# Other PSUM banks under the first attention scores, and two weight splits, two scale operations and two projection steps at other places of the order

## The chip, the cores and the metric

One core of one Trainium2 chip. The metric is the device time of one execution in microseconds (us).

## What is computed

One layer of a hybrid backbone over 512 latent tokens of width 1024, with a prefix of 256 context tokens. Cut to what matters here:

```python
hx = modulate(rms_norm(x), sh1, sc1)            # 512 tokens
hc = modulate(rms_norm(ctx), csh1, csc1)        # 256 tokens
ak, av, qkv, db, da, aq, z, gate = split_cols(h @ w_in)
q = rope(rms_norm(aq, q_norm_w)); k = rope(rms_norm(ak, k_norm_w))
attn = softmax(q @ k.T * HEAD_DIM**-0.5) @ v    # 8 heads, 2 key/value heads, 768 keys
q, k, v = silu(dwconv_centred(qkv, conv_w))     # gated DeltaNet, 8 heads, two directions
gdn = gdn_output(gdn_bidirectional(...), z)
x = x + g1 * merge_branches(attn, gdn, gate, w_pa, w_pd, w_out)
x = x + g2 * conv_ffn(modulate(rms_norm(x), sh2, sc2), w_up, ..., w_down)
return rms_norm(x, final_norm_w)
```

## The kernel before

Every product is done in three matmuls of split numbers: a weight arrives as `wraw`, ACT rounds it to `whi`, DVE takes the rest to `wlo` (`load_w`, L199; two raw buffers, three of each half), and the activations are kept in halves likewise (names ending in H and L).

PSUM has eight banks. Two (`mb`) and one (`xb`) belong to the whole program; the `xb` bank is a single one that every transposition outside the stages goes through. The other five go to one stage after the other. In the stage ahead of the key/query stage they are two `pt`, a `pm` and two `pc`. In the key/query stage (L669 to L753) they are three `pq` (the projection of a tile of 128 tokens) and two `pt` (its transposes). In the attention (L757 to L850) they are one score tile `pS` of two banks and three `ab` (transposed probabilities and values). A stage's pool gives out its banks in the order in which the code first asks for each tag.

The key/query stage has six blocks, for keys, values and four times two query heads, of six, six and four times four tiles. A tile's `pq` is accumulated in 24 matmuls; ACT squares it for the norm, DVE rotates it (`rope`, L678, six operations that read `pq` and one that adds) into `qt`, and three tiles later PE transposes `qt` into `pt` (`columns`, L688; `pend` holds what is still to be transposed). The last three tiles of the last block are transposed inside the attention, through `xb`. After a block of queries `rsqrt` and a multiplication make its scales `qsc`: a DVE operation, a power on POOL, a DVE operation.

`attend` (L821) goes through 32 units (8 heads, four tiles of 128 queries). For unit u it puts down the softmax (maximum on DVE, its product with the scale, exp on ACT with the sum, reciprocal and multiplication on DVE), then the scores of unit u + 1, which need the score tile that exp has read, then the transposes of the probabilities of unit u - 1 into `ab` (split on ACT to `PH` and on DVE to `PL`), and after every second unit the 18 value matmuls into `ab` (copied by ACT to `ao`). Between these it yields, and at each yield one step of `fillA` runs on PE: `projections` of the DeltaNet's convolution inputs, eight projections of 12 steps (eight of three 512-wide matmuls, four of six 256-wide ones, all into `mb`). `F0` to `F3` (L68) say how many steps stand at each yield; F0 stands between the first scores and the rest. ACT and DVE take a finished `mb` through the short convolution (`t1`, `co`); some steps later `tokens` (L289) transposes `co` through `xb`, where ACT copies it and squares it in place.

The order on PE is the order of the code (`pinned`). On ACT and DVE a scheduler chooses the order from its own model of times, with priorities (`first`, `sooner`). Each engine then works through its list strictly in that order, waiting at each instruction for what it needs. The load of a projection's weights stands in the program where a `wraw` buffer comes free, and its split where the scheduler puts it.

## Time and profile before

| what | us |
|---|---|
| median of 3 runs | 1256.99 |
| lowest and highest | 1254.07, 1263.17 |
| the profiled execution | 1254.9 |
| its span | 1253.1 |
| PE busy | 1193.0 (95%) |
| DVE busy | 834.0 (67%) |
| ACT busy | 613.8 (49%) |
| attention, from the first score matmul to the end of the last values | 156.31 to 327.57 |

Busy time of PE is the time in which a matmul is under way. A row of the order in time gives the start in us, the length, engine, line, operation and tiles; in brackets at its end stands how long the engine was idle just before, and what ended that. A table by windows gives the busy time and the number of instructions of each engine in a stretch, and the clock granted to TensorE as a share of the full one.

### The profile page before, as it was taken

The numbers are of one execution on the slowest core, as the hardware profiler recorded it, in microseconds if no ns is written. First come the engines' busy times: TensorE is split into PE (matmuls) and PEld (weight loads), VectorE is DVE, ScalarE is ACT, GpSimd is POOL, SyncE is SP. The second block draws the span as 40 slices with busy tenths as digits, with TensorE's granted clock in tenths as the row PEclk, the third lists the DMA queues.
The fourth block names the chain that finished last, engine by engine and source line by source line (L and its number), as shares of the span: only waits on it lengthen the run. The fifth ranks groups of instructions, "written<-read, shape, count | busy, mean of one in ns | idle before, by whom it ended". The sixth has DMA issues, their size and how long they took to land.

```text
span 1253.1 us, 20509 instructions
## 1 busy us (share of the span) xinstructions
PE 1193.0 (95%) x7733; PEld 1015.7 (81%) x7733; DVE 834.0 (67%) x1609; ACT 613.8 (49%) x1403; POOL 274.0 (22%) x347
## 2 busy tenths in 40 slices
PE   6999999999979899999999999999999999999996
PEld 3499879898768688778888678789888888888886
DVE  5666767777689866766757588855776756653333
ACT  6534466666675673773634632333544444442331
POOL 0020110110332387587484200210000000000000
PEclk9999999999999999999999999999999999999998
DMA  9412211211635533543546786763333333223331
GB/s 376 146 60 85 86 60 60 81 60 68 200 112 179 171 115 118 170 147 107 173 143 192 231 292 214 265 213 133 102 134 125 127 101 101 95 86 102 96 93 67
DMA packets 66403, 171.83 MB, mean 137 GB/s; under 512 B 7328, under 2 KB 18048, under 8 KB 64896
## 3 DMA queue, kind: packets, MB, share of 16 engines
q1 hardware_dynamic: 66304, 170.52, 41.0%
q8 instruction: 61, 1.00, 0.3%
q14 instruction: 38, 0.31, 0.1%
HBM read 145.28 MB, written 25.21 MB: 136 GB/s over the span
## 4 chain that ended last, share of the span: by engine, by line
PE 74%; DMA 7%; DVE 6%; POOL 5%; ACT 4%; issue 2%; SPq 0%; POOLq 0%; DVEq 0%; ACTq 0%
PE mc L85 33%; PE mb L85 19%; PE pq L85 6%; PE pb L85 5%; PE pS L85 3%; PE ab L85 3%; PE pm L85 2%; PE ab L89 2%; DVE wlo L106 1%; POOL NN L106 1%; DMA NN<-gamdr 1%; POOL prod L106 1%; DMA Gb<-gamdr 1%; POOL R L106 1%; PE pk L85 1%
## 5 line engine op out<-in xcount | busy, mean ns | idle before, releaser
L106 DVE TENSOR_TENSOR wlo<-wraw,whi 128x1024 fp32r<-128x1024 f32 (+1 forms) x153 | 190.5, 1246 | 150.2 <-ACT whi L118 149.5
L118 ACT ACTIVATE whi<-wraw 128x1024 fp32r<-128x1024 f32 (+1 forms) x153 | 159.6, 1045 | 216.8 <-PE mc L85 112.4
L85 PE MATMUL mc<-h,whi 128*128 128x512 f32 (+1 forms) x752 | 219.9, 376 | 0.3 <-ACT whi L118 0.3
L85 PE MATMUL mb<-hxH,whi 128*128 128x512 f32 x384 | 162.0, 422 | 5.8 <-DVE t L115 3.7
L85 PEld LDWEIGHTS mc<-h,whi 128*128 128x128 f32 x752 | 138.1, 188 | 25.9 <-ACT whi L118 0.5
L85 PE MATMUL mb<-hxH,wlo 128*128 128x512 f32 x384 | 152.0, 396 | 0.0
L85 PE MATMUL mb<-hxL,whi 128*128 128x512 f32 x384 | 151.3, 394 | 0.0
L85 PE MATMUL mc<-h,wlo 128*128 128x512 f32 (+1 forms) x376 | 141.5, 376 | 0.5 <-DVE wlo L106 0.5
L85 PE MATMUL mc<-a,whi 128*128 128x512 f32 (+1 forms) x396 | 111.2, 367 | 0.6 <-DVE x L115 0.6
L106 POOL TENSOR_TENSOR rc<-rc,mhalf 128x2 f32<-128x2 f32 x4 | 3.0, 741 | 407.8 <-DVE rc L112 407.8
L85 PEld LDWEIGHTS mb<-hxH,whi 128*128 128x128 f32 x384 | 73.4, 191 | 16.1 <-ACT t L118 4.4
L85 PEld LDWEIGHTS mb<-hxH,wlo 128*128 128x128 f32 x384 | 72.7, 189 | 16.6
L85 PEld LDWEIGHTS mc<-a,whi 128*128 128x128 f32 x396 | 71.6, 189 | 12.8 <-DVE x L115 0.8
L85 PEld LDWEIGHTS mc<-h,wlo 128*128 128x128 f32 x376 | 70.8, 188 | 13.6 <-DVE wlo L106 1.0
L85 PEld LDWEIGHTS mb<-hxL,whi 128*128 128x128 f32 x384 | 73.3, 191 | 9.5
L85 PE MATMUL mc<-a,wlo 128*128 128x512 f32 (+1 forms) x198 | 72.5, 366 | 0.0
L115 DVE SCALAR_TENSOR_TENSOR u<-mc,col,u 128x511 f32<-128x511 f32 x88 | 65.3, 746 | 1.4
L106 POOL TENSOR_TENSOR R<-R,prod 128x31 f32<-128x31 f32 (+15 forms) x93 | 57.1, 614 | 7.0
L106 POOL TENSOR_TENSOR prod<-X,R 128x31 f32<-128x31 f32 (+15 forms) x93 | 54.1, 582 | 20.2 <-DVE X L106 13.4
L85 PE MATMUL pq<-whi,hxH 128*128 128x256 f32 (+1 forms) x192 | 55.5, 289 | 0.0
L85 PE MATMUL pq<-wlo,hxH 128*128 128x256 f32 (+1 forms) x192 | 54.2, 283 | 0.1
L85 PE MATMUL pq<-whi,hxL 128*128 128x256 f32 (+1 forms) x192 | 54.1, 282 | 0.0
(329 smaller groups left out, 2759.5 us busy)
## 6 DMA issues: line engine op xcount, KB each, us to landing
wraw<-in_w_cm_dram SPq DMA_DIRECT2D x48, 512.0 KB, 3.6
wraw<-in_w_up_dram SPq DMA_DIRECT2D x44, 512.0 KB, 3.3
wl<-in_w_mod_dram SPq DMA_DIRECT2D x24, 512.0 KB, 4.3
wm<-in_w_mod_dram SPq DMA_DIRECT2D x8, 1024.0 KB, 11.2
wraw<-in_w_down_dram SPq DMA_DIRECT2D x16, 512.0 KB, 3.6
wraw<-in_w_aq_dram SPq DMA_DIRECT2D x10, 512.0 KB, 3.8
M<-gamdr SPq DMA_DIRECT2D x64, 64.0 KB, 4.7
wraw<-in_w_pa_dram SPq DMA_DIRECT2D x8, 512.0 KB, 4.4
```

The lines of the kernel that those rows point to most:

```text
L85: i = nc.tensor.matmul(*a, **k)
L89: i = nc.tensor.transpose(*a, **k)
L106: (eng or V).tensor_tensor(out=out, in0=a, in1=b, op=op)
L115: V.scalar_tensor_tensor(out=out, in0=a, scalar=s, in1=b, op0=op0, op1=op1)
L118: A.activation(out, a, f, **kw)
```

## The change

Four things, all at the passage from the key/query stage to the attention:

- The key/query stage asks for one `pt` before its first `pq` (it is used for the first tile's transposes), and the attention asks for one `ab` before its first score tile (it is used for the first probabilities). So `pt` takes the first two of the five banks and `pq` the other three; `ab` takes the first three and `pS` the last two.
- F0 is 5 in place of 3. The number of steps in all stays the same, so two steps fewer are left for the end of the attention.
- The weights of the second and third projection of the attention (`ahead`) are loaded and split after softmax(0) and after softmax(1), in the order of the code on ACT and DVE (`in_order`). In the kernel before, the scheduler had put these splits ahead of the last tile's rotation.
- The scales of the last query block are made in softmax(1) and softmax(2), in place of the end of the key/query stage.

```diff
--- before.py
+++ after.py
@@ -65,7 +65,7 @@
 AP2 = 7
 PIN = 1
 RA = .6
-F0, F1, F2, F3 = 3, 1, 1, 1
+F0, F1, F2, F3 = 5, 1, 1, 1
 AQ, AK, AM, AR = 24, 10, 32, 10
 
 C_ID, C_ONE, C_MS, C_MI, C_TRI = 0, 128, 256, 512, 768
@@ -102,20 +102,31 @@
         if dbg is not None and name in dbg:
             SP.dma_start(dbg[name], ap)
 
+    strict = [False]
+
+    def put(i):
+        return tc.keep_in_program_order(i) if strict[0] else i
+
+    def in_order(fn, *a):
+        strict[0] = True
+        r = fn(*a)
+        strict[0] = False
+        return r
+
     def tt(out, a, b, op, eng=None):
-        (eng or V).tensor_tensor(out=out, in0=a, in1=b, op=op)
+        put((eng or V).tensor_tensor(out=out, in0=a, in1=b, op=op))
 
     def ts(out, a, s1, op0, s2=None, op1=None, eng=None):
         if op1 is None:
-            (eng or V).tensor_scalar(out=out, in0=a, scalar1=s1, scalar2=None, op0=op0)
+            put((eng or V).tensor_scalar(out=out, in0=a, scalar1=s1, scalar2=None, op0=op0))
         else:
-            (eng or V).tensor_scalar(out=out, in0=a, scalar1=s1, scalar2=s2, op0=op0, op1=op1)
+            put((eng or V).tensor_scalar(out=out, in0=a, scalar1=s1, scalar2=s2, op0=op0, op1=op1))
 
     def stt(out, a, s, b, op0, op1):
-        V.scalar_tensor_tensor(out=out, in0=a, scalar=s, in1=b, op0=op0, op1=op1)
+        put(V.scalar_tensor_tensor(out=out, in0=a, scalar=s, in1=b, op0=op0, op1=op1))
 
     def act(out, a, f=AF.Copy, **kw):
-        A.activation(out, a, f, **kw)
+        put(A.activation(out, a, f, **kw))
 
     def split(hi, lo, src):
         act(hi, src)
@@ -275,8 +286,11 @@
                 act(out[:, 0:n], t1[:, 0:n], AF.Tanh, scale=0.5)
                 stt(out[:, 0:n], out[:, 0:n], 1.0, t1[:, 0:n], ALU.add, ALU.mult)
 
-        def conv_proj(tile_idx, out, with_ctx):
-            w = load_w(w_cm[tile_idx])
+        ahead = {}
+        proj_w = lambda i: w_cm[8 * order[i][1] + order[i][0]]
+
+        def conv_proj(tile_idx, out, with_ctx, w=None):
+            w = w or load_w(w_cm[tile_idx])
             off = NCX if with_ctx else 0
             n = off + NL
             t1 = stp.tile([P, NA], F32, name="t1", tag="t1", bufs=2)
@@ -335,9 +349,9 @@
                 late.pop(0)[1]()
                 n -= 1
 
-        def head_proj(h, part):
+        def head_proj(h, part, w=None):
             o = cbuf()
-            yield from conv_proj(8 * part + h, o, part != 0)
+            yield from conv_proj(8 * part + h, o, part != 0, w)
             head_out(h, part, o)
 
         def head_out(h, part, o):
@@ -417,7 +431,7 @@
 
         def projections(i0, i1):
             for i in range(i0, i1):
-                yield from head_proj(*order[i])
+                yield from head_proj(*order[i], ahead.pop(i, None))
 
         tb_es = ExitStack()
         tbp = tb_es.enter_context(tc.tile_pool(name="tbp", bufs=1, side="right"))
@@ -694,6 +708,8 @@
                 hi, lo = (KH, KL) if blk == 0 else (QH[blk - 2], QL[blk - 2])
                 split(hi[:, :, ts_], lo[:, :, ts_], pt)
 
+
+            pt1 = [kps.tile([P, 2, P], F32, name="pt", tag="pt", bufs=2)]
             pend, dec = [], decays(kvp)
             pinned[0] = KPIN
             psc = next(dec)
@@ -715,7 +731,7 @@
                         T.matmul(pq, xl[:, k, sl], hi[:, wsl], start=False, stop=False)
                         T.matmul(pq, xh[:, k, sl], lo[:, wsl], start=False, stop=(k == KT - 1))
                     if len(pend) >= LAG:
-                        columns(*pend.pop(0))
+                        columns(*pend.pop(0), *(pt1.pop() for _ in pt1[:]))
                     if (blk, t) in DAT:
                         next(dec, None)
                     if blk == 1:
@@ -743,7 +759,7 @@
                             for j in range(2):
                                 ts(qt[:, j * 128:j * 128 + 128], qt[:, j * 128:j * 128 + 128], rk[:, j:j + 1], ALU.mult)
                     pend.append((blk, t, qt))
-                if blk > 1:
+                if 1 < blk < 5:
                     rsqrt(qsc[blk - 2], qsc[blk - 2], 1.0 / HD, EPS)
                     ts(qsc[blk - 2], qsc[blk - 2], HD ** -0.5, ALU.mult)
             fillA = projections(NS, KV)
@@ -769,8 +785,10 @@
                 return pS
 
             def abank():
-                return aps.tile([P, 512], F32, name="ab", tag="ab", bufs=NB - 2)
-
+                return ab1.pop() if ab1 else aps.tile([P, 512], F32, name="ab", tag="ab", bufs=NB - 2)
+
+            ab1 = []
+            ab1.append(abank())
             hold = {}
 
             def norm(pm, r):
@@ -805,7 +823,7 @@
                         SP.dma_start(atd[h], ao)
                 return values if t % 2 == 1 else None
 
-            def softmax(h, t, pS):
+            def softmax(h, t, pS, between=None):
                 mx = at2.tile([P, 4], F32, name="mx", tag="mx", bufs=4)
                 pm = at2.tile([P, NA], F32, name="pm", tag="pm", bufs=3)
                 sc = qsc[h // 2][:, 2 * t + h % 2:2 * t + h % 2 + 1]
@@ -813,6 +831,8 @@
                     V.tensor_reduce(out=mx[:, 0:1], in_=pS[:, 0:NA], axis=AX.X, op=ALU.max)
                     stt(mx[:, 1:2], mx[:, 0:1], -1.0, sc, ALU.mult, ALU.mult)
                     act(pm, pS[:, 0:NA], AF.Exp, scale=sc, bias=mx[:, 1:2], accum_out=mx[:, 2:3])
+                if between is not None:
+                    in_order(between)
                 with first():
                     V.reciprocal(mx[:, 3:4], mx[:, 2:3])
                     norm(pm, mx[:, 3:4])
@@ -821,11 +841,15 @@
             def attend():
                 U = 4 * NH
                 at = lambda u: (u // 4, u % 4)
+                between = {1: lambda: rsqrt(qsc[3], qsc[3], 1.0 / HD, EPS),
+                           2: lambda: ts(qsc[3], qsc[3], HD ** -0.5, ALU.mult)}
                 pS, pms, pv = scores(0, 0), {}, None
                 yield F0
                 for u in range(U + 2):
                     if u < U:
-                        pms[u] = softmax(*at(u), pS)
+                        pms[u] = softmax(*at(u), pS, between.get(u))
+                        if u < 2:
+                            ahead[NS + 1 + u] = in_order(load_w, proj_w(NS + 1 + u))
                     if u + 1 < U:
                         pS = scores(*at(u + 1))
                     yield F1
```

The helpers have moved down by 11 lines, so ACT's L118 is now L129 and DVE's L106 is L117; what stands behind them moved by more. What the scheduler and the new code make of it stands in the following rows.

First place, ACT from the last squares of the key/query stage on. `qtmp` and `qsc3` are the squares of a `pq` tile, `pm` is an exp, `whi` a weight split. Before:

```order
L118 ACTIVATE whi_2156<-wraw_2155 128x1024
L118 ACTIVATE whi_2399<-wraw_2398 128x1024
L118 ACTIVATE qtmp_1927,qsc3_176<-pq_1896 128x128 x2
L118 ACTIVATE QH3_723<-pt_1921 128x2x128
L118 ACTIVATE pm_1974,mx_1973<-pS_1948,mx_1973,qsc0_173 128x768
L118 ACTIVATE QH3_723<-xb_1990 128x2x128
L118 ACTIVATE pm_2014,mx_2013<-pS_1980,mx_2013,qsc0_173 128x768
L118 ACTIVATE co_2002<-xb_2003 128x512
L118 ACTIVATE xb_2003,gkss_2001<-xb_2003 128x128 x4
L118 ACTIVATE pm_2064,mx_2063<-pS_2020,mx_2063,qsc0_173 128x768
```

and now:

```order
L129 ACTIVATE qtmp_1927,qsc3_176<-pq_1896 128x128 x2
L129 ACTIVATE QH3_723<-pt_1921 128x2x128
L129 ACTIVATE pm_1978,mx_1977<-pS_1946,mx_1977,qsc0_173 128x768
L129 ACTIVATE whi_1985<-wraw_1984 128x1024
L129 ACTIVATE co_2001<-xb_2002 128x512
L129 ACTIVATE pm_2024,mx_2023<-pS_1990,mx_2023,qsc0_173 128x768
L129 ACTIVATE whi_2033<-wraw_2032 128x1024
L129 ACTIVATE xb_2002,gkss_2000<-xb_2002 128x128 x4
L129 ACTIVATE QH3_723<-xb_2012 128x2x128
L129 ACTIVATE t1_1960<-mb_1961,col_74 128x512
L129 ACTIVATE QH3_723<-xb_2055 128x2x128
```

The two `whi` have gone from ahead of the last squares to behind exp(0) and exp(1), and the copy of `co` through `xb` has come ahead of exp(1); the transposes of `qt` (`QH3`) are read behind the four squares, not ahead of them. On DVE the two `wlo` moved in the same way: the first now stands between softmax(0) and the maximum of unit 1.

Second place, PE behind scores(1), from the end of a projection step on. Before:

```order
L85 MATMUL mb_1963<-hxH_196,wlo_1958 128x512
L89 MATMUL xb_1990<-cst_72,qt_1846 128x128 x2
L85 MATMUL mb_1963<-hxH_196,whi_1957 128x512
L85 MATMUL mb_1963<-hxL_559,whi_1957 128x512
L85 MATMUL mb_1963<-hxH_196,wlo_1958 128x512
...
L89 MATMUL xb_2003<-cst_72,co_689 128x128 x4
L85 MATMUL pS_2020<-KH_716,QH0_720 128x512
```

and now:

```order
L85 MATMUL mb_1961<-hxH_196,wlo_1956 128x512
L89 MATMUL xb_2002<-cst_72,co_689 128x128 x4
L89 MATMUL xb_2012<-cst_72,qt_1846 128x128 x2
L85 MATMUL mb_1961<-hxH_196,whi_1955 128x512
L85 MATMUL mb_1961<-hxL_639,whi_1955 128x512
...
L85 MATMUL pS_2038<-KH_716,QH0_720 128x512
```

With two more steps ahead of it, the group of four `co` transposes falls due ahead of the first pair of `qt` transposes, and both go into the one `xb` bank.

Third place, ACT in the middle of the attention, around the split of a coming projection's weights. `t1` is the convolution's first product, `PH` the split of transposed probabilities. Before:

```order
L118 ACTIVATE PH_2747<-ab_2833 128x2x128
L118 ACTIVATE xb_2815,gkss_2717<-xb_2815 128x128
L118 ACTIVATE whi_3343<-wraw_3342 128x1024
L118 ACTIVATE t1_2637<-mb_2788,col_74 128x256
L118 ACTIVATE rkk2_179<-gkss_2717,col_74 128x6
L118 ACTIVATE hk2_166<-gkss_2717,col_74 128x6
L118 ACTIVATE PH_2882<-ab_2884 128x4x128
L118 ACTIVATE PH_2882<-ab_2891 128x2x128
L118 ACTIVATE pm_2923,mx_2922<-pS_2857,mx_2922,qsc2_175 128x768
L118 ACTIVATE ao_2746<-ab_2899 128x256
```

and now:

```order
L129 ACTIVATE ao_2524<-ab_2791 128x256
L129 ACTIVATE whi_3329<-wraw_3328 128x1024
L129 ACTIVATE t1_2623<-mb_2752,col_74 128x256
L129 ACTIVATE PH_2760<-ab_2838 128x4x128
L129 ACTIVATE pm_2872,mx_2871<-pS_2825,mx_2871,qsc1_174 128x768
L129 ACTIVATE PH_2760<-ab_2845 128x2x128
L129 ACTIVATE co_2616<-t1_2623 128x768
L129 ACTIVATE PH_2888<-ab_2890 128x4x128
L129 ACTIVATE PH_2888<-ab_2897 128x2x128
L129 ACTIVATE pm_2929,mx_2928<-pS_2878,mx_2928,qsc2_175 128x768
```

Before, five instructions stand between the split and the next exp, two of `PH` among them; now two do, and the exp behind them belongs to the unit in which the last context step of a projection runs.

## Prediction

> **What bounds the kernel now.** I read the page's chain first, then the waits of PE stage by stage, then the order in time of PE, DVE and ACT around 156 us. The chain that ended last is PE for three quarters:
>
> ```profile
> PE 74%; DMA 7%; DVE 6%; POOL 5%; ACT 4%; issue 2%; SPq 0%; POOLq 0%; DVEq 0%; ACTq 0%
> ```
>
> So a stall of PE counts in full, and work that only moves on ACT or DVE counts where PE comes to wait for it. The stages around the change, as busy time of each engine by window (columns: length; busy us and instructions of PE, PEld, DVE, ACT, POOL; granted clock; DMA):
>
> ```profile
> 153.30:156.30 3.00, 0.00 (x0) 0.01 (x1) 2.88 (x9) 1.54 (x6) 0.00 (x0) 1.00 0.43 132
> 156.30:158.70 2.40, 2.38 (x7) 2.12 (x8) 0.86 (x4) 0.00 (x0) 1.64 (x1) 0.50 0.73 263
> 190.00:310.00 120.00, 120.00 (x816) 108.97 (x816) 91.62 (x178) 77.50 (x186) 7.05 (x4) 1.00 0.19 70
> ```
>
> Three microseconds without a matmul, then 2.4 us in which every matmul ran at a granted clock of 0.50; and later 120.00 us of PE in 120.00. In the attention's steady state nothing can be won on PE, and every new wait there is a loss. The transition itself on PE:
>
> ```profile
> 152.91 0.38 PE L89 MATMUL pt<-cst,qt 128*128 128x128 f32 x2
> 156.31 0.77 PE L85 MATMUL pS<-KH,QH 128*128 128x512 f32 x1 [3.02 <-DVE qsc L112]
> 161.07 0.44 PE L85 MATMUL pS<-KH,QH 128*128 128x512 f32 x1
> 162.18 0.39 PE L85 MATMUL mb<-hxH,whi 128*128 128x512 f32 x1
> 162.88 0.38 PE L89 MATMUL xb<-cst,qt 128*128 128x128 f32 x2
> ...
> 164.49 0.60 PE L89 MATMUL xb<-cst,co 128*128 128x128 f32 x4
> 164.84 0.48 PE L85 MATMUL pS<-KH,QH 128*128 128x512 f32 x1
> ...
> 167.37 0.44 PE L89 MATMUL xb<-cst,qt 128*128 128x128 f32 x2 [0.54 <-ACT xb L118]
> ...
> 173.15 0.44 PE L89 MATMUL xb<-cst,qt 128*128 128x128 f32 x2 [1.27 <-ACT xb L118]
> ...
> 175.94 0.39 PE L85 MATMUL pS<-KH,QH 128*128 128x512 f32 x1
> ```
>
> On DVE and on ACT in the same stretch:
>
> ```profile
> 150.85 0.42 DVE L106 TENSOR_TENSOR qt<-pq,qA 128x256 f32<-128x256 f32 x1 [1.35 <-ACT qtmp L118]
> ...
> 152.73 2.58 DVE L106 TENSOR_TENSOR wlo<-wraw,whi 128x1024 fp32r<-128x1024 f32 x2 [0.27 <-ACT whi L118]
> ...
> 156.49 0.42 DVE L106 TENSOR_TENSOR qt<-qt,qtmp 128x256 f32<-128x256 f32 x1
> ...
> 158.61 0.96 DVE L813 TENSOR_REDUCE mx<-pS 128x1 f32<-128x768 f32 x1 [0.38 <-PE pS L85]
> ...
> 162.38 0.96 DVE L813 TENSOR_REDUCE mx<-pS 128x1 f32<-128x768 f32 x1 [0.56 <-PE pS L85]
> ```
>
> ```profile
> 150.19 0.28 ACT L118 ACTIVATE qtmp<-pq 128x128 f32<-128x128 f32 x1 [2.07 <-issue]
> ...
> 153.00 1.06 ACT L118 ACTIVATE whi<-wraw 128x1024 fp32r<-128x1024 f32 x1 [0.29 <-PE pq L85]
> ...
> 159.88 0.99 ACT L118 ACTIVATE pm<-pS,mx,qsc 128x768 f32<-128x768 f32 x1 [5.05 <-DVE mx L115]
> ...
> 165.12 0.60 ACT L118 ACTIVATE co<-xb 128x512 f32<-128x512 f32 x1 [0.47 <-PE xb L89]
> 165.75 0.26 ACT L118 ACTIVATE xb<-xb 128x128 f32<-128x128 f32 x1
> ```
>
> The first score matmul waited for the read of the last query block's last tile (PE's wait is put down to the small `qsc` operation just behind that read). That tile's rotary multiply stood behind two `wlo` (152.73, 2.58 us), and its squares on ACT behind a `whi` (153.00). The stall costs 3.0 us of idleness; and from 156.31 to 161.07 a score tile and three filler steps took 4.76 us, where at full clock they take 1.11 (161.07 to 162.18) + 3 x 0.70 (162.18 to 162.88) = 3.2. With the slow clock the stall is worth 3.0 + 1.6 = **4.6 us**. That is all that the change can win.
>
> **The change, part by part.**
>
> *The banks.* The pools take banks in the order in which tags are first used. In the old kernel three `pq` banks come first and the score tile lies over two of them; 28 `pq` tiles rotate, so the last one lies in the first bank, under the scores. Now `pt` comes first, `pq` is the stage's third to fifth bank, `ab` the first three, and the scores lie over the fourth and fifth: the second and third tile of the last block. The third tile's rotary multiply began at 150.85, two microseconds before PE's transposes at 152.91, which end at about 153.3. The old wait goes: scores(0) start at 153.3.
>
> The early price: `pq` now begins on banks that the stage before held, and its second tile has to wait for a conv read of bank `pc`:
>
> ```profile
> 69.64 0.47 DVE L115 SCALAR_TENSOR_TENSOR t<-pc,col,t 128x255 f32<-128x255 f32 x1
> ...
> 70.28 0.28 PE L85 MATMUL pq<-whi,hcH 128*128 128x256 f32 x1
> ```
>
> That read ends at 70.11; the second tile starts at 70.28: nothing to 0.1 us; I take 0.05.
>
> *The head start.* Without splits ahead of it, DVE does the last rotation from about 153.85 (0.66 after the squares, as 150.19 to 150.85) to 155.45 (1.6 long: in the old kernel it began when the `wlo` were done, at 155.3, and its last piece, 156.49, ended at 156.91). The first maximum follows at 155.4; exp starts 1.27 later (158.61 to 159.88), the next scores 1.19 after that (159.88 to 161.07): at 157.85. PE has 1.1 + 5 x 0.70 = 4.6 us of work from 153.3, to 157.9. So scores(1) start 3.2 us earlier than the old 161.07, with two more steps (1.4 us) done: all 4.6 us, at that point.
>
> *What the moved splits meet.* ACT's order is now exp(0), `whi`, copy of `xb`, exp(1), `whi`, four squares of `xb`; DVE's is `wlo`, max(1). PE, after scores(1) and one step, reaches the four `co` transposes into the single `xb` bank at 159.65 and at 160.0 the two `qt` transposes into the same bank, which wait for the fourth square. In the old order `qt` came first and the `co` transposes were two steps later (162.88, 164.49). Now: exp(0) 156.65 to 157.75; `whi` (1.06) to 158.8; `wlo` (half of 2.58, 1.25) to 160.05; max(1) behind it although the scores are there at 159.15 (1.31 after their start, 161.07 to 162.38); exp(1) at 161.25; the second `whi` at 162.3 to 163.35; the squares take 1.6 (165.75 to PE's return at 167.37). PE goes on at **164.95, after 4.95 us of idleness**. At 164.84 the old kernel had done the same matmuls and one pair of transposes more: the gain is given back to the last tenth. What is behind the wait on PE is everything, so it counts in full.
>
> That stall is longer than the one that lowered the clock at 156. How idleness and clock go together elsewhere in this trace:
>
> ```profile
> 364.00:366.00 2.00, 0.00 (x0) 0.00 (x1) 2.00 (x5) 1.36 (x3) 1.17 (x1) 1.00 0.00 0
> 366.00:368.20 2.20, 2.17 (x11) 1.80 (x12) 2.20 (x6) 0.29 (x2) 0.00 (x0) 1.00 0.75 196
> 375.00:377.30 2.30, 0.36 (x4) 0.19 (x2) 2.27 (x6) 1.89 (x6) 0.00 (x0) 1.00 0.53 130
> 377.30:379.30 2.00, 2.00 (x7) 1.46 (x8) 1.90 (x5) 0.00 (x0) 0.69 (x1) 0.71 0.12 48
> ```
>
> After 2.1 us of idleness (364 to 366) the clock stayed at 1.00, after 1.9 us (375 to 377) it fell to 0.71, after 3.0 us to 0.50. After 4.95 us I count the fall as the likelier, at the same 1.6 us; bounds nothing and 1.6.
>
> The Trainium skill, "TensorE: Matmul & The Clock Gate", section "HAM oscillation — how this bites in real kernels", asks for no gap of PE above about 3.4 us. By that rule the old gap would have cost no clock and the new one would, so the change would lose 1.6 us more than it does by the rows. The trace disagrees on the old gap (3.02 us, clock 0.50), so I keep the rows' sum.
>
> The same bank gives two more waits before scores(4). The pair of `co` transposes has its squares behind exp(2), two PH copies and the co copy: about 1.6 us. The third `qt` waits for the fourth square of the next four, with `whi` of the fifth projection put between the third and the fourth: about 2.1 us. The old kernel has 0.54 (167.37) and 1.27 (173.15) there. Adding up PE's work from 164.95 (two score tiles, eight steps, twelve transposes of probabilities, the `xb` pairs) with these waits and the clock, scores(4) start at about 180.8 with two steps more done; the old start was 175.94, plus those two steps 177.3. **Head: +3.5 us**, from +1.9 (no fall of the clock) down to -4.6 (the `xb` wait absent) as bounds.
>
> *Steady state.* Two steps of head start shift the filler's phase by two against the units. A projection has 12 steps, a period of four units uses 12, so one phase holds for the rest. The `whi` of a coming projection needs a weight buffer, which the last context matmul of the projection under way gives back. In the old order that falls into a long unit with 18 value matmuls. In the new one it falls into the shortest unit: scores, one context step, six transposes, two steps. There ACT has `whi`, `t1`, `PH` ahead of exp. Rows for both sides:
>
> ```profile
> 247.13 1.00 ACT L118 ACTIVATE pm<-pS,mx,qsc 128x768 f32<-128x768 f32 x1
> ...
> 320.00 1.07 ACT L118 ACTIVATE whi<-wraw 128x1024 fp32r<-128x1024 f32 x1
> 320.95 0.48 ACT L118 ACTIVATE t<-mb,col 128x256 f32<-128x256 f32 x1
> 321.30 0.61 ACT L118 ACTIVATE PH<-ab 128x512 fp32r<-128x512 f32 x1
> 321.78 0.32 ACT L118 ACTIVATE rkk<-gkss,col 128x6 f32<-128x6 f32 x1
> ```
>
> ```profile
> 243.99 0.40 PE L85 MATMUL pS<-KH,QH 128*128 128x512 f32 x1
> ...
> 248.27 0.50 PE L85 MATMUL pS<-KH,QH 128*128 128x512 f32 x1
> ...
> 315.26 0.40 PE L85 MATMUL pS<-KH,QH 128*128 128x512 f32 x1
> ...
> 323.37 0.88 PE L89 MATMUL ab<-cst,pm 128*128 128x128 f32 x6 [0.29 <-DVE PL L106]
> ...
> 327.57 0.40 PE L85 MATMUL mb<-hxH,whi 128*128 128x512 f32 x1
> ```
>
> PE's work in the short unit, s being its start: 243.99 to 248.27 is 4.28, less four transposes (0.48), with a context step for a step of the same length: 3.8. The buffer is free at s + 1.1 + 0.7 (scores and step, as at 161.07), `whi` starts at s + 1.9, exp 1.78 later (320.00 to 321.78, the same three instructions), the next scores 1.14 after that (247.13 to 248.27): s + 4.8. PE stands for 1.0 us, six times (once a projection): **+6.0 us**. Lower bound nothing (if `whi` gets away earlier), upper bound 1.3 each, 8.
>
> *Tail.* The steps that ran early are missing at the end. From the last scores to the end of the attention takes 315.26 to 327.57 = 12.3 us, with three steps and two transposes in it. Now one step is left, but the chain hardly shortens: exp(31) at s + 3.7 stands behind the same `whi`, `t1` and `PH`, its transposes wait for DVE and for the values of the pair before until some s + 7.9, and from those transposes to the end is 4.2 (323.37 to 327.57): 12.1. The stretch is 0.2 shorter and 1.4 of steps have left it: **+1.2**, bounds 0 and 1.6.
>
> *The query scales* (0.16 + 0.17 us on DVE, a POOL power between) are needed first by unit 24, a hundred microseconds later: nothing. The weight loads keep their sequence on the queue; two start later by some 6 us, and the projections that use them start 8 us and more after that: nothing, at worst 1.
>
> **Sum** against the profiled execution: 1254.9 + 0.05 + 3.5 + 6.0 + 1.2 = 1265.65; I name **1265.5**. The median of the runs shown is 1257.0, 2.1 above that execution, so the range leans upwards.
>
> **Rivals.**
>
> *The gain stays.* If the four squares come before the second `whi` in effect, or the steps cover them, the head keeps -4.6 and the shifted units hide their `whi`: 1250.3. For it: the removed wait is certain in the trace. Against it: ACT takes its instructions in order, and the moved `whi` is written ahead of the squares. Chance 0.12.
>
> *Head as said, units free.* The six short units do not stall, because exp needs only 4.28 - 1.14 = 3.1 us in a short unit of the old kernel and the buffer may be free earlier than I put it: 1254.9 + 3.5 + 1.2 = 1259.6. Against it: the new order has `whi` ahead of exp, and 1.9 + 1.78 is 3.7. Chance 0.22.
>
> *More clock.* Stalls of 1.6 and 2.1 us in the head each lower the clock as the 1.9 us at 375 did (1.6 us each), and the short units cost 1.3: 1265.65 + 3.2 + 1.8 = 1270.6. It is slower by over 1% from about 1269.6 on. Chance 0.16.
>
> *The wait is not removed.* Another read of the last tile still holds scores(0): the old 4.6 stays and the later waits of the head shrink by about as much: about 1265. The rotation of banks speaks against it. Chance 0.03.
>
> The Trainium skill, "Perfetto Trace Analysis", section "Matmuls", wants independent matmul groups to rotate through different PSUM banks, so that the emptying of one lies beside the next. The one `xb` bank breaks it: the row 173.15 with its 1.27 us agrees, and the sum above has that wait in it already.
>
> **How the numbers follow.** Forecast 0.47, rivals 0.12, 0.22, 0.16, 0.03. A measurement of this kernel tells about 1% (12.6 us) from no change. Faster by that much needs more than the 4.6 us that there are: 0.02. Slower by it: most of the third rival and a tenth of the forecast, 0.18. Range 1251 to 1273: it leaves out most of the first rival and the top of the third. Slower cases hold most of the chance; the forecast's own range is 1260 to 1270.
>
> **What would show it.** Right: scores(0) at 153.3 with no wait named `qsc`; scores(1) near 157.9; a wait of PE `xb` for ACT of 4 to 5 us near 160; a clock of 0.5 behind it; six waits of `pS` for ACT `pm` of about 1 us each, 20 us apart; PE less than 120 of 120 between 190 and 310. Wrong: no long `xb` wait (then the first rival), or PE full in the steady state (the second).

## The result, and the profile after

| | before | changed |
|---|---|---|
| median, us (6 runs each, side by side) | 1259.95 | 1274.39 |
| lowest and highest | 1254.07, 1263.17 | 1271.27, 1278.81 |
| the profiled execution | 1254.9 | 1277.77 |
| its span | 1253.1 | 1276.0 |

The ratio is 1.0113 [1.0093, 1.0133]: slower by 14.4 us. The forecast was 1265.5, with a range up to 1273.

PE's waits between 150 and 345 us in the profile after (in all, times, longest, us). The wait for `qsc` is gone, and in its place stand the two that the prediction named, `xb` and `pS`:

```profile
PE xb L89 <- ACT xb L129: 7.1, 3, 4.4
PE pS L85 <- ACT pm L129: 5.7, 10, 0.8
PE ab L89 <- DVE PL L117: 2.2, 1, 2.2
PE ab L85 <- DVE PL L117: 0.7, 2, 0.3
```

PE in order of time after, from the last transposes of the key/query stage to the fifth score tile:

```profile
153.37 0.38 PE L89 MATMUL pt<-cst,qt 128*128 128x128 f32 x2
153.51 0.48 PE L85 MATMUL pS<-KH,QH 128*128 128x512 f32 x1
158.21 0.50 PE L85 MATMUL pS<-KH,QH 128*128 128x512 f32 x1
...
165.02 0.69 PE L89 MATMUL xb<-cst,qt 128*128 128x128 f32 x2 [4.37 <-ACT xb L129]
167.98 0.39 PE L85 MATMUL pS<-KH,QH 128*128 128x512 f32 x1
...
171.96 0.44 PE L89 MATMUL xb<-cst,co 128*128 128x128 f32 x2 [0.46 <-DVE QL L117]
174.50 0.97 PE L89 MATMUL xb<-cst,co 128*128 128x128 f32 x4 [1.40 <-ACT xb L129]
175.12 0.77 PE L85 MATMUL pS<-KH,QH 128*128 128x512 f32 x1
179.78 0.44 PE L89 MATMUL xb<-cst,qt 128*128 128x128 f32 x2 [1.31 <-ACT xb L129]
182.10 0.40 PE L85 MATMUL pS<-KH,QH 128*128 128x512 f32 x1
```

The scores follow the transposes at once (153.37, 153.51), scores(1) come at 158.21, and then PE stands for 4.37 us before the pair of `qt`. ACT in that stretch shows why:

```profile
161.46 0.99 ACT L129 ACTIVATE pm<-pS,mx,qsc 128x768 f32<-128x768 f32 x1 [0.18 <-DVE mx L126]
162.35 0.19 ACT L129 ACTIVATION_READ_ACCUMULATOR pm<-pS,mx,qsc 128x1 f32 x1
162.44 1.04 ACT L129 ACTIVATE whi<-wraw 128x1024 fp32r<-128x1024 f32 x1
163.39 0.27 ACT L129 ACTIVATE xb<-xb 128x128 f32<-128x128 f32 x1
...
164.60 0.26 ACT L129 ACTIVATE xb<-xb 128x128 f32<-128x128 f32 x1
```

Exp, the second `whi`, then the four squares that keep the bank: the predicted order. By windows (length; busy us and instructions of PE, PEld, DVE, ACT, POOL; granted clock; DMA):

```profile
161.05:164.46 3.41, 0.00 (x0) 0.00 (x0) 2.15 (x6) 3.17 (x10) 1.78 (x1) 1.00 0.48 154
164.46:167.87 3.41, 2.85 (x8) 2.37 (x9) 0.71 (x2) 0.86 (x5) 0.00 (x0) 0.50 0.48 154
171.29:174.70 3.41, 1.55 (x12) 1.15 (x12) 2.29 (x8) 3.07 (x11) 0.00 (x0) 1.00 0.06 23
174.70:178.11 3.41, 3.41 (x15) 3.12 (x14) 0.69 (x1) 1.97 (x9) 2.61 (x2) 0.50 0.23 92
182.10:330.00 147.90, 142.24 (x957) 126.91 (x956) 101.75 (x206) 91.14 (x228) 10.05 (x8) 1.00 0.18 67
331.71:335.13 3.42, 1.34 (x9) 1.11 (x10) 3.42 (x8) 3.13 (x7) 0.00 (x0) 1.00 0.45 153
335.13:338.54 3.41, 3.41 (x18) 3.41 (x17) 1.37 (x3) 0.39 (x1) 0.00 (x0) 0.50 0.29 115
```

The windows are laid on the moments at which the clock changes. It is 0.50 behind the long wait, as predicted, and 0.50 twice more, from 174.70 and from 335.13, where nothing was predicted. PE, which had 120.00 of 120.00 in the steady stage, now lacks 5.7 of 147.9. A short unit there, on PE and on ACT:

```profile
199.39 0.39 PE L85 MATMUL pS<-KH,QH 128*128 128x512 f32 x1
...
204.15 0.50 PE L85 MATMUL pS<-KH,QH 128*128 128x512 f32 x1 [0.80 <-ACT pm L129]
```

```profile
201.22 1.06 ACT L129 ACTIVATE whi<-wraw 128x1024 fp32r<-128x1024 f32 x1 [1.96 <-PE mb L85]
202.19 0.46 ACT L129 ACTIVATE t<-mb,col 128x256 f32<-128x256 f32 x1
202.54 0.59 ACT L129 ACTIVATE PH<-ab 128x512 fp32r<-128x512 f32 x1
203.02 0.99 ACT L129 ACTIVATE pm<-pS,mx,qsc 128x768 f32<-128x768 f32 x1
```

From scores to scores 4.76 us; predicted 4.8. `whi`, `t`, `PH` stand ahead of exp as foreseen. The tail, last scores at 328.25 and the first matmul behind the attention at 342.11:

```profile
328.25 0.39 PE L85 MATMUL pS<-KH,QH 128*128 128x512 f32 x1
...
333.45 0.44 PE L89 MATMUL ab<-cst,pm 128*128 128x128 f32 x2 [2.19 <-DVE PL L117]
...
342.11 0.39 PE L85 MATMUL mb<-hxH,whi 128*128 128x512 f32 x1
```

**Where the 14.4 us are.** I cut the attention of each profile into three by PE's rows: head, from the end of the last `pt` transposes to scores(4); steady, to scores(31); tail, to the first matmul behind the attention. Before: 153.29 to 175.94, to 315.26, to 327.57. After: 153.75, 182.10, 328.25, 342.11. The two steps (0.70 us each) that the changed kernel does in the head and not in the tail are taken from the one and given to the other. That makes head 28.35 - 22.65 - 1.4 = **+4.3**, steady 146.15 - 139.32 = **+6.8**, tail 13.86 - 12.31 + 1.4 = **+2.95**: 14.1 in all, against 14.4 between the medians. The two profiled executions are 22.9 apart, because that of before stands 5.05 below its own median and that of after 3.4 above; behind the attention the spans differ without any edit there. From its end to the first matmul `pb<-S,kT` of the next stage it is 125.0 us before, 128.1 after, and 128.0 in e7 below, whose order on PE is that of before. The granted clock goes with that: it stood at 0.50 for 6.8 us of this stretch before, and for 13.7 us in both of the others.

### The profile page after: what moved, and what is told of

It is laid out like the page before. It is cut to its first block, busy times and chain, and to the rows that moved or that the text cites. A ratio compares the mean times of both kernels' runs of the same rounds, so it can differ in the third digit from the quotient of the medians.

```text
span 1276.0 us, 20509 instructions
## 1 busy us (share of the span) xinstructions
PE 1208.4 (95%) x7733; PEld 1025.4 (80%) x7733; DVE 831.7 (65%) x1609; ACT 614.9 (48%) x1403; POOL 270.9 (21%) x347
## 4 chain that ended last, share of the span: by engine, by line
PE 70%; DVE 10%; DMA 7%; ACT 5%; POOL 4%; issue 3%; SPq 0%; POOLq 0%; DVEq 0%; ACTq 0%
PE mc L85 32%; PE mb L85 17%; PE pq L85 6%; PE pb L85 4%; PE ab L85 3%; PE pS L85 3%; DVE wlo L117 2%; DMA wl<-in_w_mod_dram 2%; PE pm L85 2%; ACT whi L129 1%; POOL prod L117 1%; PE ab L89 1%; PE pk L85 1%; POOL R L117 1%; ACT pm L129 1%
## 5 line engine op out<-in xcount | busy, mean ns | idle before, releaser
L117 DVE TENSOR_TENSOR wlo<-wraw,whi 128x1024 fp32r<-128x1024 f32 (+1 forms) x153 | 192.8, 1261 | 157.8 <-ACT whi L129 156.6
L129 ACT ACTIVATE whi<-wraw 128x1024 fp32r<-128x1024 f32 (+1 forms) x153 | 159.4, 1043 | 233.7 <-PE mc L85 112.8
L117 POOL TENSOR_TENSOR rc<-rc,mhalf 128x2 f32<-128x2 f32 x4 | 3.3, 813 | 407.5 <-DVE rc L123 407.5
L117 POOL TENSOR_TENSOR R<-R,prod 128x31 f32<-128x31 f32 (+15 forms) x93 | 57.1, 614 | 7.0
L117 POOL TENSOR_TENSOR prod<-X,R 128x31 f32<-128x31 f32 (+15 forms) x93 | 54.1, 581 | 20.7 <-DVE X L117 14.0
```

The costliest lines, as they stand in the source:

```text
L117: put((eng or V).tensor_tensor(out=out, in0=a, in1=b, op=op))
L129: put(A.activation(out, a, f, **kw))
```

## The experiments

**Theory A**: the two steps of head start are the whole loss. They decide which transposes take the `xb` bank first, where the next `whi` falls among a unit's exponentials, and what is left for the tail. Rival **B**: the moved splits cost it, by holding up exp and the squares. Rival **C**: the banks cost it, the score tile having no work beside it once it starts early. Other rivals are told in the expectations that bring them in. Differences from before by the same three stages, worked out as above with 0.70 us for each step moved from the stage. Each ratio is to runs of the kernel before made side by side (medians 1259.95 for the changed kernel, 1261.21 for e1 to e4, 1260.30 for e5 to e8, 1259.92 for e9 and e10, 1260.58 for e11 and e12). The stages are from one profile each, and a fall of the clock in one of them is worth up to 1.7 us:

| run | F0 | median, us | ratio to before | attention | head | steady | tail |
|---|---|---|---|---|---|---|---|
| changed | 5 | 1274.39 | 1.0113 [1.0093, 1.0133] | +14.1 | +4.3 | +6.8 | +2.95 |
| e1 | 3 | 1257.63 | 0.9980 [0.9959, 1.0002] | -2.0 | -2.0 | 0.0 | 0.0 |
| e2 | 5 | 1274.80 | 1.0110 [1.0087, 1.0132] | +14.9 | +6.65 | +6.8 | +1.4 |
| e3 | 5 | 1262.85 | 1.0017 [1.0000, 1.0033] | +2.7 | +2.9 | -0.2 | 0.0 |
| e4 | 5 | 1264.71 | 1.0022 [1.0005, 1.0039] | +1.8 | +0.2 | +2.2 | -0.6 |
| e5 | 5 | 1262.78 | 1.0015 [0.9994, 1.0036] | -1.4 | -4.1 | +3.35 | -0.6 |
| e6 | 5 | 1262.37 | 1.0011 [0.9989, 1.0033] | -1.55 | -5.7 | +4.8 | -0.6 |
| e7 | 3 | 1263.22 | 1.0016 [0.9998, 1.0033] | +0.8 | +0.8 | 0.0 | 0.0 |
| e8 | 5 | 1271.56 | 1.0096 [1.0068, 1.0125] | +11.6 | +3.4 | +6.8 | +1.45 |
| e9 | 5 | 1259.17 | 0.9986 [0.9967, 1.0005] | -2.2 | -5.7 | +3.5 | 0.0 |
| e10 | 3 | 1258.03 | 0.9991 [0.9970, 1.0013] | -3.3 | -2.9 | -0.4 | 0.0 |
| e11 | 4 | 1263.32 | 1.0021 [1.0003, 1.0038] | +2.4 | +1.1 | +0.9 | +0.3 |
| e12 | 6 | 1270.83 | 1.0076 [1.0048, 1.0104] | +10.4 | +1.2 | +8.3 | +0.95 |

**e1: the change without the head start.**

```diff
-F0, F1, F2, F3 = 5, 1, 1, 1
+F0, F1, F2, F3 = 3, 1, 1, 1
```

> The changed kernel with F0 back at 3 (new banks, moved splits and scales stay). Theory A (the two steps more in the head are what costs: they put the co transposes ahead of the qt transposes in the one xb bank, shift the phase of the fillers by two steps for all of the attention, and are missing at its end): all three losses go, no waits of 1 us of pS for ACT pm in the steady state, and of the removed wait some 2 us remain as a gain: 2 us below the kernel before (ratio 0.998), 14 to 16 us below the changed one. Theory B (the two moved splits cost, since they stand ahead of exp(1) and of the xb squares): the long xb wait stays, 4 us or more above the kernel before. Theory C (the new banks cost): as slow as the changed kernel.

Measured: 1257.63. PE's waits in the head:

```profile
157.25 0.50 PE L85 MATMUL pS<-KH,QH 128*128 128x512 f32 x1 [1.33 <-ACT pm L129]
161.85 0.50 PE L85 MATMUL pS<-KH,QH 128*128 128x512 f32 x1 [0.52 <-ACT pm L129]
164.88 0.44 PE L89 MATMUL xb<-cst,qt 128*128 128x128 f32 x2 [1.03 <-ACT xb L129]
...
170.66 0.44 PE L89 MATMUL xb<-cst,qt 128*128 128x128 f32 x2 [1.27 <-ACT xb L129]
```

Four short ones, behind which the clock stayed at 1.00, and steady and tail to 0.02 us those of before. Banks, splits and scales together are no loss: as A expected, against B and C.

**e2: the kernel before with the head start alone.**

```diff
-F0, F1, F2, F3 = 3, 1, 1, 1
+F0, F1, F2, F3 = 5, 1, 1, 1
```

> The kernel before with only F0 changed from 3 to 5. Theory A: about as slow as the changed kernel or up to 3 us more, 12 to 17 us above the kernel before (the wait for qsc stays, the xb wait is about 3 us, the phase costs 6 to 7 us, the tail 3). Theories B and C: neither splits nor banks have moved, so within 2 us of the kernel before.

Measured: 1274.80, the loss of the whole change. Here the wait for `qsc` is still there, and the one for `xb` comes on top:

```profile
PE pS L85 <- ACT pm L118: 5.7, 10, 0.8
PE xb L89 <- ACT xb L118: 5.6, 3, 3.1
PE pS L85 <- DVE qsc L112: 3.0, 1, 3.0
PE ab L89 <- DVE PL L106: 2.2, 1, 2.2
```

The 5.7 of `pS` and the 2.2 of `ab` are those of the changed kernel to the tenth: they belong to the two steps and to nothing else.

**e3: the two steps are given back after the head**, so that the steady stage has the old phase.

```diff
-                    yield F3
+                    yield 0 if u in (3, 5) else F3
```

> The changed kernel with one filler step left out in units 3 and 5 (both have value matmuls), so that from unit 6 on the fillers stand as in the kernel before; the head with its xb wait stays. Theory A: no waits of pS for ACT pm behind 200 us, tail as before: 9 to 10 us below the changed kernel, 4 to 5 us above the kernel before. Theory B or C: the phase is no matter, within 2 us of the changed kernel.

Measured: 1262.85. Steady -0.2, tail 0.0, and in the head the long wait as it was:

```profile
164.09 0.69 PE L89 MATMUL xb<-cst,qt 128*128 128x128 f32 x2 [4.37 <-ACT xb L129]
```

So the phase is the cause of the 6.8 and of the tail; the loss of the head stays. A had 4 to 5 us above before; the median is 1.6 above. e4, e5 and e8 look at the order in the `xb` bank.

**e4: e3 with later transposes of the projection** (`AK`, the age at which `tokens` runs; a step counts two).

```diff
-AQ, AK, AM, AR = 24, 10, 32, 10
+AQ, AK, AM, AR = 24, 14, 32, 10
```

> As the run before, and the age at which token transposes fall due raised by two steps (AK 10 to 14), so that the qt transposes come first again in the xb bank. Theory A: the xb wait of 4 us falls below 1.5 us and the head keeps 2 to 4 us of the removed wait: 2 to 4 us below the kernel before. Theory B: the xb wait stays near 4 us, since the splits still stand ahead of exp(1) and the squares: as e3. Theory C: as the changed kernel.

Measured: 1264.71, no gain over e3, and 3.5 us above before where A had 2 to 4 below. The first wait fell to 1.58, nearly as meant, but the next pair of `co` now came ahead of the third pair of `qt`, and made the same kind of wait there:

```profile
165.47 0.44 PE L89 MATMUL xb<-cst,qt 128*128 128x128 f32 x2 [1.58 <-ACT xb L129]
173.09 0.69 PE L89 MATMUL xb<-cst,qt 128*128 128x128 f32 x2 [3.10 <-ACT xb L129]
```

**e5: e4 with that pair of `co` put off (`AP2`); e6: the splits behind softmax(1) and softmax(3) too.**

```diff
-AP2 = 7
+AP2 = 9
```

```diff
-                        if u < 2:
-                            ahead[NS + 1 + u] = in_order(load_w, proj_w(NS + 1 + u))
+                        if u in (1, 3):
+                            ahead[NS + 1 + u // 2] = in_order(load_w, proj_w(NS + 1 + u // 2))
```

> The run with the phase put back and tokens two steps later, and the second piece of a token transposition one step later still (AP2 7 to 9), so that all three qt pairs go through the xb bank ahead of a group of squares, not behind one. Theory A (what waits in the single xb bank decides the head): the wait of 3.1 us of the run before and the low clock behind it go, about 4 us less than that run, 1 to 2 us below the kernel before. Theory D (the order in the bank is no matter, the split of the fifth projection on ACT holds the same place anyway): a wait of about 3 us stays somewhere before 180 us, no change from the run before.

> As e5, and the two splits moved further back, behind softmax(1) and softmax(3) in place of softmax(0) and softmax(1). Theory A with the splits as a smaller part: the maximum of unit 1 no longer stands behind wlo, scores(2) start about 1 us earlier, 1 to 2 us less than e5, 3 us below the kernel before. Theory B (the splits are the main loss): more than 4 us less than e5.

Measured: 1262.78 and 1262.37, 2.5 and 2.1 us above before, so A's times are missed in both. The long `xb` wait is gone and the head is won (-4.1 and -5.7), which is against D, but the later ages hold through the whole attention and behind it: steady +3.35 and +4.8 (in part work of the head that only moved), and from the end of the attention to `pb<-S,kT` 133.75 and 132.0 us, where before has 125.0 and e7 128.0. For 20.5 and 23.9 us of that the clock stood at 0.50 (before 6.8), so much of it is clock. The attention is 1.4 and 1.55 shorter, and the time is not.

**e7: the banks alone, in the kernel before.**

```diff
+            pt1 = [kps.tile([P, 2, P], F32, name="pt", tag="pt", bufs=2)]
-                        columns(*pend.pop(0))
+                        columns(*pend.pop(0), *(pt1.pop() for _ in pt1[:]))
-                return aps.tile([P, 512], F32, name="ab", tag="ab", bufs=NB - 2)
+                return ab1.pop() if ab1 else aps.tile([P, 512], F32, name="ab", tag="ab", bufs=NB - 2)
+            ab1 = []
+            ab1.append(abank())
```

> The kernel before with only the banks changed (F0 3, splits and scales where they were). Theory A: scores(0) start at 153.3 without a wait, but on DVE the first maximum still stands behind two wlo, the rotation and the second scale operation that waits for POOL, so exp(0) is at most 0.4 us earlier and the wait comes back at scores(1) as 4 us for ACT pm: within 1.5 us of the kernel before. Theory E (the wait for the bank was the whole stall): 4 to 5 us below the kernel before. Theory C (the banks cost): above it by 4 us or more.

Measured: 1263.22, no gain: against E, and 2.9 us above before where A had at most 1.5. The wait has moved by one score tile:

```profile
160.61 0.80 PE L85 MATMUL pS<-KH,QH 128*128 128x512 f32 x1 [4.13 <-ACT pm L129]
```

```profile
160.50:163.50 3.00, 2.89 (x8) 2.46 (x9) 1.35 (x3) 0.06 (x1) 0.00 (x0) 0.50 0.03 5
```

Scores(0) start early, three steps follow, and scores(1) wait for exp(0), which stands behind the splits. The banks alone are worth nothing: e1, which has the moved splits and scales as well, is 2.8 us of the attention below e7. About 1.4 of that is the fall of the clock behind the 4.13.

**e8: the change with the splits left to the scheduler.**

```diff
-                        if u < 2:
-                            ahead[NS + 1 + u] = in_order(load_w, proj_w(NS + 1 + u))
```

> The changed kernel with the two splits back where the scheduler puts them, ahead of the last rotation (banks, F0 5 and scales as changed). Theory A: scores(1) about 1.5 us later than in the changed kernel, the xb wait about 1 us shorter, phase and tail as there: within 2 us of the changed kernel, 12 to 16 us above the kernel before. Theory B: no more than 4 us above the kernel before.

Measured: 1271.56, 11.3 above before, a little under A's 12 to 16 and far from B's 4. The steady waits and the tail's are there unchanged, and so is an `xb` wait:

```profile
157.11 0.50 PE L85 MATMUL pS<-KH,QH 128*128 128x512 f32 x1 [1.36 <-ACT pm L129]
162.69 0.69 PE L89 MATMUL xb<-cst,qt 128*128 128x128 f32 x2 [3.14 <-ACT xb L129]
```

The moved `whi` makes that wait 1.2 us longer (4.37); the order in the bank makes the rest of it, since in e5, with another order in the bank and the splits where the changed kernel has them, the longest wait for `xb` in the head is 1.58. B falls but for this 1.2.

**e9: e6 with the old ages put back after the head.**

```diff
-                late.insert(0, (tick[0] + AP2, lambda: (piece(4, 2), finish())))
+                late.insert(0, (tick[0] + second[0], lambda: (piece(4, 2), finish())))
...
+                    if u == 2:
+                        age[0], second[0] = 10, 7
```

> As e6, but the later token ages hold only until unit 2 and are the old ones from there on, so that the steady state, the tail and what comes behind the attention stand as in the kernel before. Theory A: scores(4) as early as in e6 (18 to 19 us after the last transposes of the stage ahead), 137 to 138 us from there to scores(31), tail 12.3, behind the attention 125 to 128 us as in the kernel before: the attention 5 to 6 us shorter than before, 4 to 6 us below the kernel before (ratio 0.996). Theory F (what the head gains is lost again behind the attention whatever its order, since there the DeltaNet's chain over POOL and DMA sets the end): within 2 us of the kernel before.

Measured: 1259.17, ratio 0.9986, 0.75 us below before: A's 4 to 6 are missed, and the time is F's. The span behind the attention is nearly as before (126.8 for 125.0, with the clock at 0.50 for 10.2 us of it), but of the head's -5.7 the steady stage gives 3.5 back, in part as work that only moved, and in a wait of 1.88 for `xb` at 188.19 (before has 0.88 there), where the transposes that were put off come close upon the next ones.

**e10: e1 with the splits behind softmax(1) and softmax(3)** (the edits of e1 and e6).

> As e1 (F0 3, banks and scales as changed), with the splits moved behind softmax(1) and softmax(3). Theory A: the wait of 1.3 us at scores(1) stays, the one of 0.5 at scores(2) and some of the first xb wait go: 1 us less than e1, 3 to 4 us below the kernel before. Theory F: within 2 us of the kernel before.

Measured: 1258.03. The shortest attention of all, 3.3 us under before, and in the time 1.9 us that the interval [0.9970, 1.0013] does not tell from nothing. A had 3 to 4; F, within 2 us of before, fits this number and that of e9, and no run here tests its reason.

**e11 and e12: a head start of 4 and of 6 in the changed kernel.** Is it the number of steps, or where they fall?

```diff
-F0, F1, F2, F3 = 5, 1, 1, 1
+F0, F1, F2, F3 = 4, 1, 1, 1
```

```diff
-F0, F1, F2, F3 = 5, 1, 1, 1
+F0, F1, F2, F3 = 6, 1, 1, 1
```

> The changed kernel with a head start of 4 of the weight units' steps instead of 5. Theory A (what decides is where a filler step puts whi and t1 among ScalarE's exponentials and evictions): with 4 the transpositions of q take the xb bank ahead of those of the projection, and whi stands behind the unit's exponentials in the steady stage, so the stalls of 0.80 us in every third unit are gone: steady stage 139 to 141 us (before 139.3, changed 146.2), tail at most 13.0, time 0.997 to 1.002 of before. Rival G (each further step of head start costs in proportion, from nothing at 3 to 14 us at 5): 7 us above before, 1.0055, steady stage near 143.

> The changed kernel with a head start of 6 steps instead of 5. Theory A: the six stalls of 0.80 us in the steady stage are away or fewer, since the steps fall on other units, so at most 142 us there; the projection's transpositions still hold the xb bank ahead of those of q, so the head is as late as in the changed kernel or later, and the tail has 1.4 us less of steps to lie beside: 4 to 9 us above before, ratio 1.003 to 1.007, less than the changed kernel's 1.011. Rival G (in proportion to the steps): 21 us above before, 1.017, steady stage near 149.

Measured: 1263.32 and 1270.83. With 3, 4, 5 and 6 steps the attention differs from before by -2.0, +2.4, +14.1 and +10.4: no price for each step, so G falls. With 4 no unit stalls in the steady stage (140.3 us), as A had it, and the ratio of 1.0021 is at the edge of A's 1.002; the head's gain is lost to one long `xb` wait that A had not foreseen:

```profile
174.16 0.69 PE L89 MATMUL xb<-cst,qt 128*128 128x128 f32 x2 [3.14 <-ACT xb L129]
```

With 6, A is missed: 1.0076 is above its 1.007, it expected fewer stalls in the steady stage and at most 142 us there, and there are six of 1.02 to 1.08 us and 147.6 us; the head is 3.1 us shorter than in the changed kernel, where A had it as long or longer. ACT's exp is now free of `whi`, but DVE has `wlo` between the maximum and its product with the scale. DVE and PE in one such unit:

```profile
219.45 0.96 DVE L831 TENSOR_REDUCE mx<-pS 128x1 f32<-128x768 f32 x1 [2.05 <-PE pS L85]
220.32 1.22 DVE L117 TENSOR_TENSOR wlo<-wraw,whi 128x1024 fp32r<-128x1024 f32 x1
221.46 0.48 DVE L126 SCALAR_TENSOR_TENSOR t<-mb,col,t 128x255 f32<-128x255 f32 x1
221.85 0.15 DVE L126 SCALAR_TENSOR_TENSOR mx<-mx,qsc 128x1 f32<-128x1 f32 x1
```

```profile
223.23 0.50 PE L85 MATMUL pS<-KH,QH 128*128 128x512 f32 x1 [1.08 <-ACT pm L129]
```

So a split that falls into a short unit holds up exp on either engine, by its first half on ACT or its second on DVE.

## Why the prediction was wrong

The direction and the mechanism were right: the `qsc` wait went, an `xb` wait took its place, the short units stalled by the predicted order of ACT, and e2 shows the two steps alone to cost as much as the whole change. The size was not. The forecast is 8.9 us under the measured median, from two terms: the base of the sum, and falls of the clock that the sum does not have.

**The base: 5.05 us.** The sum was added to the profiled execution, 1254.9, and the named time was that sum. The median of before in the comparison is 1259.95, and 1261.21 over 29 runs beside e1; the step "the median of the runs shown is 1257.0, 2.1 above that execution, so the range leans upwards" saw the offset, moved only the range by it, and took it too small. The three times shown reached 1263.17, 8 above the execution profiled. The granted clock goes with this offset: the profiled execution had 0.989 over its span, and of 98 runs of the same kernel beside the experiments one had more. Of these, the 38 with 0.983 or less have a median of 1262.8, and the 28 with 0.986 or more one of 1258.4. So the base was an execution with few falls of the clock.

**The terms: 3.8 us** (14.4 measured, 10.65 summed; 14.1 in the profiles).

- *Banks.* Right: scores(0) at 153.51, on the heels of the transposes. The early price, 0.05, is not to be told from the spread: with the same banks scores(0) start at 151.01 in e8 and at 153.51 here.
- *Head start.* Right: scores(1) start 4.46 us after the transposes' end; predicted 4.55.
- *Head, +3.5: measured +4.3.* The waits were 4.37, 0.46, 1.40 and 1.31, 7.5 in all, for the 4.95, 1.6 and 2.1 of the prediction, 8.65. The fall of the clock behind the long wait came as counted and cost 1.4 (2.85 us of PE at 0.50). Not counted was the second one, 3.41 us of PE at 0.50 from 174.70, which cost 1.7. Against before, which has 4.8 of waits and one fall of 1.7 here, that is 2.7 of waits and 1.4 of clock, 4.1 of the 4.3.
- *Steady, +6.0: measured +6.8.* The six short units are right: 4.76 us from scores to scores, of which 3.80 are PE's own work as predicted (199.39 to 203.19, where the next matmul could have started), so 0.96 each. The profile calls 0.80 of that idle, because the last matmul ahead of a wait is shown with its full 0.40 us, where the next one starts after 0.23 in a row. Four waits of 0.20 to 0.22 were in units that I had not looked at. The waits sum to 5.7, where before has one of 0.88 in this stage (`xb`, at 186.93); with 0.17 for each that makes 6.3. About 0.5 is not resolved.
- *Tail, +1.2: measured +2.95.* The chain is the one described, and where the clock held, the term is right to 0.25: e2 and e8 have the same 2.19 us wait and +1.45. In the changed kernel's profile the clock fell to 0.50 from 335.13 on, which is 1.5 us more. The bounds 0 to 1.6 had no clock in them.
- *Scales and loads, nothing.* Right: e1 has both, and no wait for either.

The failed steps are thus the base, 5.05 us, and the term for the clock, which was counted as one fall in the head that takes the place of the old one; the two falls that were not counted cost 1.7 and 1.5, 3.2 of the 3.8. Behind the second lies a reading: the rows at 364 and 375 were taken as the length of one wait and the clock after it, and 0.71 as a level that the clock took. It was a mean: between 377.30 and 379.30 the clock is 1.00 up to 378.15 and 0.50 from there. What decides is told in the last section, and by it the two falls were bad luck: the same wait in the tail of e2 brought none, and the same series of waits in the head of e3 (1.32 and 1.34 behind the 4.37) no second one.

"More clock" was the rival nearest to the result, with the right price of about 1.6 us a fall but too low a base; it had both further falls in the head, where there was one, and 1.3 for a short unit. "The gain stays" fell with the 4.37 of `xb`, and "units free" with the 5.7 of `pS`.

What stays open: the change without its head start (e1, e10) has an attention 2.0 to 3.3 us shorter in the profiles and medians 3.6 and 1.9 us lower, but both intervals hold 1, so that it beats the kernel before is likely and not shown. Rival F, that such a gain is lost again behind the attention, is not excluded.

## What to carry to other kernels

Work that fills the gaps of a pipeline has a phase: moving two steps of it changes no amount of work, but here it put a weight split ahead of the exponential in each short unit, which cost more than the 4.6 us stall that was being removed. Before moving filler, write down the order of each engine that reads PSUM for one whole period, and the order in which work enters a single-buffered bank. Add a sum to the median of several runs, not to one profiled execution. And read the granted clock in short windows: a mean of 0.76 over 7 us was 3.4 us at 0.50.

## What the runs showed of the hardware

The granted clock does not follow the length of the last wait. In these fourteen traces it has two values, 1.00 and 0.50; what lies between is the mean of a window in which it changed. Within a trace it changes only at marks that are 3.41 us or a whole multiple of that apart, to 0.01 us. In the changed kernel it fell at 164.46, 174.70 and 335.13, which is 3 and 47 times 3.41 us apart, and rose again 3.41 us after each.

Whether it falls at a mark goes with how busy PE was since the mark before. Of the stretches that begin between 150 and 345 us at 1.00, over all the traces, every one with PE busy for up to 1.55 us is followed by 0.50 (18 of them, the one ahead of 174.70 the busiest), and none with PE busy for 1.57 us or more (the least busy is that from 186.34 to 189.76 in e9). This is read from these traces and tested by no run of its own, and the limit is not the same everywhere: around 515 us there are falls behind stretches that were busy for 53% and 56% (e11, e4).

So several short waits count together: between 171.29 and 174.70 they were 0.46 and 1.40. And one wait counts by how the marks cut it. The 2.19 us of the changed kernel's tail lie mostly in the stretch from 331.71, busy for 1.34, and the clock fell. In e2 a mark, by their spacing, falls into the same wait (333.28 to 335.47), which leaves 2.16 and 2.13 busy on its two sides, and the clock stayed:

```profile
331.12:334.53 3.41, 2.16 (x20) 1.92 (x18) 2.45 (x4) 2.43 (x4) 1.55 (x3) 1.00 0.18 68
334.53:337.94 3.41, 2.13 (x16) 1.89 (x17) 3.41 (x8) 2.33 (x6) 0.00 (x0) 1.00 0.47 154
```

Where the marks lie against the work differs from trace to trace, and no edit here sets it. A fall costs up to half of 3.41 us. The stretch from the end of the attention to `pb<-S,kT` shows the price: 125.0 us with 6.8 us at 0.50 (before), 126.6 and 126.8 with 10.2 (e1, e9), 128.0 to 128.1 with 13.7 (the changed kernel, e7, e10), some 1.5 for each further 3.4.

The Trainium skill, "TensorE: Matmul & The Clock Gate", section "A second HAM failure mode: psum-queue depth-cycling", tells of a kernel that cycles through PSUM banks and in which TensorE idles shortly between groups of matmuls so often that its clock goes down and up. The trace agrees in kind (waits of 0.46 and 1.40 us, then the clock at 0.50). The same page's rule of about 3.4 us for a single gap, in "HAM oscillation — how this bites in real kernels", does not cover these runs: waits of 2.19 (the changed kernel's tail), 3.02, 3.10 and 3.14 us lowered the clock to 0.50.
